# Projection fill written ahead of the rows in the differential-attention units of a Trainium2 block kernel

## The chip, the cores and the metric

The kernel is one program on one core of a Trainium2 chip. A core has engines with instruction streams of their own: TensorE (PE, with its weight loads shown as PEld), VectorE (DVE), ScalarE (ACT), GpSimd (POOL) and SyncE (SP), which here issues nearly all DMAs. The metric is the device time of one execution in microseconds (us), as the median of several runs.

## The reference

One decoder block with S = 1024 tokens and width 1024. A normalised input is projected; 8 forgetting-attention (FoX) heads and 4 differential-attention heads run over the projections; their outputs are gated, projected, merged by sigmoid gates, projected again and added to the input. The part in which the change lies is the differential attention:

```python
qd = apply_rope(qb.reshape(b, s, DIFF_HEADS, 2, DIFF_QK_DIM).transpose(0, 2, 3, 1, 4), cos, sin)
kd = apply_rope(kb.reshape(b, s, DIFF_HEADS, 2, DIFF_QK_DIM).transpose(0, 2, 3, 1, 4), cos, sin)
# diff_attention, for a block i of 128 query rows:
logits = jnp.einsum('bhmqd,bhmkd->bhmqk', qi, k).astype(jnp.float32) * scale
logits = jnp.where(kpos[None, :] <= qpos[:, None], logits, -jnp.inf)
p = jax.nn.softmax(logits, axis=-1)
pd = p[:, :, 0] - lam * p[:, :, 1]
return jnp.einsum('bhqk,bhkd->bhqd', pd.astype(v.dtype), v)
```

FoX attention is alike, with one softmax per head and a cumulated forget term added to the logits.

## The kernel before

All values are fp32. For TensorE each is split into a high and a low part in fp32r, and each matrix product is done as three products (high by high, high by low, low by high); a projection chunk of 512 columns is 24 matmuls. The phases follow one another on the clock: the normalised input and the value projections up to about 107 us, the projections of the first unit up to 131 us, then eight attention units, then gates, branch products and output products to the end.

A unit is a differential head (units 0 to 3) or a pair of FoX heads (units 4 to 7). A unit has groups of two rows, a row being 128 queries. For a differential row the function `row` asks for the swapped copies X of the query operand (L473, DMAs from SP), calls `s_row` for each of the two softmaxes (score matmuls L492 and L493 into a PSUM tile `Sd`; a DVE read of that tile with mask and running extreme into `Pd` and `mxd`, L495; an exponential on ACT, L501), takes the reciprocals `l` (DVE, L591), scales the second softmax on POOL (L592) and the first on ACT (L594), and adds them on POOL (L595). A group's `products` are built by `av`: transposes of `Pd` on PE into `ptd` (L522), a cast on ACT into `phd` (L525), the low part on DVE into `pld` (L526), the products with V on PE into `ypd` (L546), and an evacuation. Row i of a unit has (i+1) x 128 columns, and a score tile at most 512, so late rows cost more; the four groups g = 0 to 3 carry the weights 3, 7, 11 and 15, of 36.

Beside its rows and products each unit has a `fill`: the projections of the next unit, cut into chunks (k and q, two each), a z chunk (`pz`), and from unit 3 on sums of squares (`ssq`). A projection loads its weights by a DMA (L314, `raw_k` and the like), splits them on POOL (`hi_k`, L321) and DVE (`lo_k`, L324), runs 24 matmuls (L334) into one of two PSUM tiles `pk`, `pq` or `pz`, and for a differential unit goes through a rotation (`rope`): a copy on ACT (L362), four DMAs for the swapped halves (L366), a product on DVE (L368) and one on POOL (`swk`, `swq`, L369), their sum on DVE (L370), and the stacking into TA, TB, KA, KB (L378 to L382 with DMAs; L384 to L387 in unit 0). How much of the fill is taken behind a group goes by the weights done so far: units 0 and 1 have 6 tasks and take 1, 1, 2, 2; unit 2 has 4 and takes 1 each; unit 3 has 9 and takes 1, 2, 3, 3.

The pools that bear on the order: three PSUM tiles for scores, two for projections, two for transposes and one for `ypd`; two buffers each for the raw, high and low weights; a pool of three large buffers that holds the rotation tables and the mask and later the forget rows `cb` of FoX units (`cb` is loaded at L578 and trimmed on POOL at L618).

The written order of a unit's group n is: rows of n, products of group n-1, share n of the fill. This is not the order of execution. The code is recorded and a list scheduler in the tool chain then sets each engine's instruction order by a simulated timeline, with the written order as priority. Two things written the other way round can therefore come out interleaved in many ways, and a change at one place moves instructions on every engine behind it.

Of the kernel before, what the change touches and what calls it, by code (L numbers as in the profile page):

```python
# [50 lines left out]
def tile_hybrid_block(  # L51
# [288 lines left out]
    with ExitStack() as st:  # L340
# [75 lines left out]
        def z_tasks(t):  # L416
            return spill_tasks(f"z{t}", (ZA + t * P) if t < 4 else (ZB + (t - 4) * P), z_d[t])
# [20 lines left out]
        def sum_squares(t, c):  # L438

            sl = slice(c * CH, (c + 1) * CH)  # L440
            sq = stg.tile([P, CH], F32, tag="raw", name=f"sq{t}_{c}", bufs=4)
            nc.sync.dma_start(sq, y_d[t][:, sl])
            nc.scalar.activation(sq, sq, AF.Square)
            hi, lo = (stg.tile([P, CH], F32R, tag="sw", name=f"sq{part}{t}_{c}") for part in range(2))
            nc.scalar.copy(hi, sq)
            nc.gpsimd.tensor_tensor(lo, sq, hi, op=ALU.subtract)
            ps = pj.tile([P, CH], F32, tag="pj", name=f"ssq{t}_{c}")[0:32]
            nc.tensor.matmul(ps, lhsT=onesr, rhs=hi, start=True, stop=False)
            nc.tensor.matmul(ps, lhsT=onesr, rhs=lo, start=False, stop=True)
            nc.scalar.copy(sq[0:1], ps[0:1])  # L450
            nc.sync.dma_start(ss_d[t:t + 1, sl], sq[0:1])

        def subln_scales(t):
            rs = sub_rs[:, t]
            nc.sync.dma_start(rs, ss_d[t].rearrange("(p j) -> p j", j=8))
            rstd_of(rs, rs, P, SUB_EPS)
            nc.sync.dma_start(rs_d[t].rearrange("(p j) -> p j", j=8), rs)
# [96 lines left out]
        def products(trans, prod, g):  # L554
            for jj in range(g + 1 + SKEW):
                if jj <= g:
                    trans(jj)
                if jj >= SKEW:
                    prod(jj - SKEW)
# [91 lines left out]
        def forget_sums():  # L651

            fgf = fg.rearrange("p a b -> p (a b)")
            fs = pp.tile([P, 4, 64], F32, tag="P", name="fs")
            fn, fe, fu, fc = (fs[:, n, :] for n in range(4))
            nc.vector.tensor_scalar(fn, fgf, -1.0, None, op0=ALU.mult)
            nc.vector.tensor_tensor(fn, fn, fgf, op=ALU.min)
            nc.scalar.activation(fe, fn, AF.Exp)
            nc.vector.tensor_scalar(fu, fe, 1.0, None, op0=ALU.add)
            nc.vector.tensor_scalar(fc, fu, -1.0, None, op0=ALU.add)  # L660
            nc.vector.tensor_tensor(fc, fe, fc, op=ALU.subtract)
            nc.scalar.activation(fn, fu, AF.Ln)
            nc.vector.reciprocal(fu, fu)
            nc.vector.tensor_tensor(fc, fc, fu, op=ALU.mult)
            nc.vector.tensor_tensor(fn, fn, fc, op=ALU.add)
            nc.vector.tensor_scalar(fe, fgf, 0.0, None, op0=ALU.min)
            nc.vector.tensor_tensor(fe, fe, fn, op=ALU.subtract)
            lf = pp.tile([8, S], F32, tag="P", name="lf")
            cum = pp.tile([8, S], F32, tag="P", name="cum")
            ones8 = pp.tile([8, S], F32, tag="P", name="ones8")  # L670
            nc.gpsimd.memset(ones8, 1.0)
            for half in range(2):
                tp = tps.tile([P, CH], F32, tag="tp", name=f"ft{half}")
                for q in range(4):
                        b = half * 4 + q
                        nc.tensor.transpose(tp[0:8, q * P:(q + 1) * P], fe[:, b * 8:(b + 1) * 8], ident)
                nc.scalar.copy(lf[:, half * CH:(half + 1) * CH], tp[0:8, :])
            nc.vector.tensor_tensor_scan(cum, ones8, lf, initial=0.0, op0=ALU.mult, op1=ALU.add)
            nc.vector.tensor_scalar(cum, cum, -8.0, None, op0=ALU.mult)
            nc.sync.dma_start(cum_d, cum)  # L680
# [7 lines left out]
        for u in range(8):  # L688
            load, load_v, groups = nxt or unit_attn(u, T)
            nxt = None  # L690
            if u == 0:
                vload.append(load_v)
            if u == 1:
                forget_sums()
            load()
            fill = []
            if u + 1 < 8:
                T, tasks = unit_proj(u + 1)
                fill += tasks
            for t in ZFILL[u]:  # L700
                fill += z_tasks(t)
            for t in SFILL[u]:
                fill += [lambda t=t, c=c: sum_squares(t, c) for c in range(2)]
                fill.append(lambda t=t: subln_scales(t))
            late = [fill.pop(), gate[0]] if u == 7 else []
            total = sum(s[0] for s in groups)
            done, nf = 0, 0
            for n, (wgt, rws, prd) in enumerate(groups):
                if n == len(groups) // 2 and u < 7:
                    nxt = unit_attn(u + 1, T)  # L710
                    vload.append(nxt[1])
                for r in rws:
                    r()
                mark = lasts[0]
                if pend and (u < 7 or n <= TAIL):
                    products(*pend())
                if u == 7 and n >= TAIL:
                    tail.append(prd)
                pend = prd
                done += wgt  # L720
                while nf < len(fill) and nf < len(fill) * done * (3 if u == 7 else 1) / total:
                    fill[nf]()
                    nf += 1
                if u == 7:
                    for f, a, b in LATE[n]:
                        with tc.issue_after(mark):
                            late[f](range(a, b))
                    if n == GFILL:
                        break
# [503 lines left out]
```

## Time and profile before

| what | value |
|---|---|
| runs | 900.85, 901.63, 899.52 us; median 900.85 |
| profiled execution | 899.54 us, of which the span of the trace is 897.8 |
| granted TensorE clock, mean | 0.998 |
| first differential unit (0) | about 131 to 181 us of the span |
| units 1 and 2, and the start of 3 | 181 to 297 us |
| rest of unit 3 | 297 to 333 us |
| FoX units 4 to 7 | 333 to 582 us and a little beyond |
| gates, branch and output products | 582 us to the end |

The profiled execution is 1.74 us longer than its span and 1.31 us below the median of the three runs. Where the profile gives a row `[x <-engine ...]`, x is the idle time in front of that instruction and what follows the arrow is what ended it. PEld is the part of TensorE that loads weights ahead of the matmuls: it can wait while earlier matmuls still run, so a wait shown on PEld is more than what the matmuls lose by it.

### The profile page before, as it was taken

How to read it: one execution, taken by the hardware profiler on the slowest of the kernel's cores; microseconds unless marked ns; L12 is line 12 of the kernel's file. 1: busy time of each engine (PE TensorE's matmuls, PEld its weight loads, DVE VectorE, ACT ScalarE, POOL GpSimd, SP SyncE). 2: the span in 40 equal slices, each digit the busy share in tenths (PEclk: the TensorE clock that was granted, in tenths of full speed). 3: DMA queues.
4: the chain of work that ended last, by engine and by line, in shares of the span. 5: the costliest groups of instructions: out<-in, count | busy, mean ns of one | idle time of the engine just before them, and what ended most of it. 6: DMA issues, size and time to landing. Idle time of an engine off the chain costs nothing.

```text
span 897.8 us, 13825 instructions
## 1 busy us (share of the span) xinstructions
PE 881.9 (98%) x4612; PEld 746.7 (83%) x4612; DVE 580.4 (65%) x1124; ACT 429.0 (48%) x864; POOL 408.9 (46%) x401
## 2 busy tenths in 40 slices
PE   8999999999999999999999999999999999999997
PEld 6999987788888888888888888888888888888885
DVE  6666555767666744456647556626776897648896
ACT  7423224665756654365545646624453362314352
POOL 2234224645646535254344435426534323483963
PEclk9999999999999999999999999999999999999999
DMA  8576656756657763635636430297766599210495
GB/s 306 188 254 245 215 164 158 179 137 170 155 137 184 183 177 77 187 94 133 188 94 155 141 106 30 88 411 240 235 202 213 168 359 312 78 41 1 123 197 172
DMA packets 138186, 154.81 MB, mean 172 GB/s; under 512 B 12145, under 2 KB 98161, under 8 KB 137090
## 3 DMA queue, kind: packets, MB, share of 16 engines
q1 hardware_dynamic: 133744, 151.55, 56.1%
q0 software_dynamic: 4224, 2.10, 2.1%
q8 instruction: 37, 0.61, 0.3%
q14 instruction: 35, 0.29, 0.1%
q10 hardware_dynamic: 146, 0.27, 0.1%
HBM read 86.17 MB, written 38.34 MB: 139 GB/s over the span
## 4 chain that ended last, share of the span: by engine, by line
PE 87%; DMA 3%; DVE 3%; SPq 2%; ACT 2%; POOL 2%; issue 1%; POOLq 0%; DVEq 0%; ACTq 0%
PE x_g L830 15%; PE pv L214 10%; PE pb L990 10%; PE pz L334 9%; PE x_o L830 8%; PE pk L334 7%; PE pq L334 7%; PE ypf L546 3%; PE ptf L522 3%; PE ypd L546 2%; PE Sf L492 2%; PE Sf L493 2%; PE ptd L522 1%; PE Sd L492 1%; PE Sd L493 1%
## 5 line engine op out<-in xcount | busy, mean ns | idle before, releaser
L214 PE MATMUL pv<-wvhi,hT 128*128 128x264 f32 (+2 forms) x384 | 88.6, 325 | 0.0
L334 PE MATMUL pq<-hT,hi_q 128*128 128x512 f32 x256 | 82.1, 395 | 0.0
L334 PE MATMUL pz<-hT,hi_z 128*128 128x512 f32 x256 | 81.6, 394 | 0.4 <-DVE rotq L368 0.3
L334 PE MATMUL pk<-hT,hi_k 128*128 128x512 f32 x256 | 81.7, 393 | 0.0
L990 PE MATMUL pb<-yT,hi_br 128*128 128x512 f32 x256 | 79.0, 389 | 0.0
L830 PE MATMUL x_g<-T,a_g 128*128 128x512 f32 x336 | 78.0, 391 | 0.0
L830 PE MATMUL x_o<-wo_op,a_o 128*128 128x512 f32 x324 | 74.8, 392 | 0.0
L830 PEld LDWEIGHTS x_g<-T,a_g 128*128 128x128 f32 x336 | 63.1, 188 | 13.8
L830 PEld LDWEIGHTS x_o<-wo_op,a_o 128*128 128x128 f32 x324 | 60.7, 188 | 13.9 <-DVE a_o L767 0.5
L214 PEld LDWEIGHTS pv<-wvhi,hT 128*128 128x128 f32 x384 | 64.8, 192 | 5.7
L526 DVE TENSOR_TENSOR plf<-ptf,phf 128x512 fp32r<-128x512 f32 (+1 forms) x80 | 50.1, 635 | 25.1 <-ACT phf L525 24.4
L501 ACT ACTIVATE Pd<-Pd,mxd 128x128 f32<-128x128 f32 (+7 forms) x64 | 49.8, 779 | 33.4 <-DVE mxd L495 33.3
L618 POOL TENSOR_TENSOR cb<-cb,trim 128x128 f32<-128x128 f32 x64 | 29.3, 462 | 74.6 <-DVE mxf L495 51.6
L214 PE MATMUL pv<-wvlo,hT 128*128 128x256 f32 (+2 forms) x192 | 61.7, 326 | 0.0
L501 ACT ACTIVATE Pf<-Pf,mxf 128x1024 f32<-128x1024 f32 (+3 forms) x64 | 49.8, 779 | 24.5 <-DVE mxf L495 22.4
L830 PE MATMUL x_g<-hT,a_g 128*128 128x512 f32 x252 | 59.1, 392 | 0.0
L623 POOL TENSOR_SCALAR Pf<-Pf,lf 128x1024 f32<-128x1024 f32 (+3 forms) x64 | 47.9, 753 | 20.9 <-DVE lf L622 17.6
L525 ACT CAST phf<-ptf 128x512 fp32r<-128x512 f32 (+1 forms) x80 | 42.6, 543 | 30.7 <-PE ptf L522 26.4
L990 PEld LDWEIGHTS pb<-yT,hi_br 128*128 128x128 f32 x256 | 48.0, 188 | 10.4 <-issue 0.4
L830 PEld LDWEIGHTS x_g<-hT,a_g 128*128 128x128 f32 x252 | 47.3, 188 | 10.4
L334 PEld LDWEIGHTS pz<-hT,hi_z 128*128 128x128 f32 x256 | 47.3, 188 | 9.5 <-DVE rotq L368 0.6
L334 PEld LDWEIGHTS pq<-hT,hi_q 128*128 128x128 f32 x256 | 47.2, 188 | 8.9
(277 smaller groups left out, 2289.2 us busy)
## 6 DMA issues: line engine op xcount, KB each, us to landing
t_d<-t SPq DMA_DIRECT2D x16, 512.0 KB, 4.0
T<-t_d SPq DMA_DIRECT2D x8, 1024.0 KB, 11.0
raw<-in_w_in_dram SPq DMA_DIRECT2D x14, 512.0 KB, 5.5
vb_d<-vbs SPq DMA_DIRECT2D x8, 512.0 KB
va_d<-vas SPq DMA_DIRECT2D x8, 512.0 KB, 3.8
raw_k<-in_w_in_dram SPq DMA_DIRECT2D x8, 512.0 KB, 4.4
raw_q<-in_w_in_dram SPq DMA_DIRECT2D x8, 512.0 KB, 4.7
V<-vb_d SPq DMA_DIRECT2D x4, 1024.0 KB, 6.2
```

The lines of the kernel that those rows point to most:

```text
L214: nc.tensor.matmul(ps[n], lhsT=hT[hp][k // 4][i // 4][:, k % 4, hs], rhs=wt[k][:, a:b], start=first, stop=(k == KT - 1 and hp == 1))
L334: mm = nc.tensor.matmul(ps, lhsT=a[:, k, :], rhs=hT[h][k // 4][c][:, k % 4, :], start=(k == 0 and a is hi and h == 0), stop=(k == KT - 1 a ...
L492: nc.tensor.matmul(ps, lhsT=A[:, qs], rhs=B[:, a:b], start=True, stop=False)
L501: nc.scalar.activation(pr[:, 0:n], pr[:, 0:n], AF.Exp, bias=mx[:, len(pcs) - 1:len(pcs)], scale=-1.0, accum_out=le)
L522: lasts[0] = nc.tensor.transpose(pt[:, o * P:(o + 1) * P], rows[2 * g + r][:, j * P:(j + 1) * P], ident).ins
L525: nc.scalar.copy(ph[:, 0:n], pt[:, 0:n])
L526: nc.vector.tensor_tensor(pl[:, 0:n], pt[:, 0:n], ph[:, 0:n], op=ALU.subtract)
L546: lasts[0] = nc.tensor.matmul(o, lhsT=a, rhs=b[:, src], start=(j == 0 and n == 0), stop=(odd == 1 and jj == g and n == len(prods) - 1)).ins
L618: nc.gpsimd.tensor_tensor(diag, diag, trim, op=ALU.add)
L623: held[0] = nc.gpsimd.tensor_scalar(p1[:, 0:n], p1[:, 0:n], l1, 1.0, op0=ALU.mult, op1=ALU.mult).ins
L830: nc.tensor.matmul(x[m], lhsT=a[:, ai, k, :], rhs=right[m][bi][k], start=(k == 0 and n == 0), stop=(k == 3 and n == 2))
L990: nc.tensor.matmul(ps, lhsT=a[:, kk, :], rhs=yT[g][h][:, k % 2, sl], start=(k == 0 and a is hi and h == 0), stop=(k == 3 and a is lo))
```

## The change

For units 0 to 3 the share of the fill that belongs to a group is written in front of the group's rows. The sum of the weights done is raised earlier, so the share itself is the same, and the second call behind the products then finds nothing left. For units 4 to 7 the written order is the one of before. A unit's written order becomes: fill 0, rows 0, products of the unit before; fill 1, rows 1, products 0; and so on. Between units 3 and 4 the fill of unit 3 now stands before its last rows, and the fill of unit 4 still behind its first.

```diff
--- before.py
+++ after.py
@@ -709,6 +709,16 @@
                 if n == len(groups) // 2 and u < 7:
                     nxt = unit_attn(u + 1, T)
                     vload.append(nxt[1])
+                done += wgt
+
+                def more(nf):
+                    while nf < len(fill) and nf < len(fill) * done * (3 if u == 7 else 1) / total:
+                        fill[nf]()
+                        nf += 1
+                    return nf
+
+                if u < 4:
+                    nf = more(nf)
                 for r in rws:
                     r()
                 mark = lasts[0]
@@ -717,10 +727,7 @@
                 if u == 7 and n >= TAIL:
                     tail.append(prd)
                 pend = prd
-                done += wgt
-                while nf < len(fill) and nf < len(fill) * done * (3 if u == 7 else 1) / total:
-                    fill[nf]()
-                    nf += 1
+                nf = more(nf)
                 if u == 7:
                     for f, a, b in LATE[n]:
                         with tc.issue_after(mark):
```

Nothing is added or removed on any engine: the number of PE, DVE, ACT, POOL and SP instructions and their shapes are the same. The order of all engines is the same up to about 131 us and from about 629 us of the time before, and differs between.

The first place is VectorE in unit 0, around rows 4 and 5 (`loq1_0` and `rotk1_1` belong to the projection of unit 1). `Pd0_1_4<-Sd0_1_4_0` is the read of the first score tile of row 4, second softmax, of unit 0; `lo_k2` is the low part of the key weights of unit 2. Before:

```order
L379 TENSOR_TENSOR loq1_0_1657<-rotq1_0_1652,hiq1_0_1656 128x512
L495 ISA Pd0_1_4_1684,mxd0_1_4_1685<-Sd0_1_4_0_1686,dmask_168 128x384
L495 ISA mxd0_1_4_1685 128x1
L368 TENSOR_TENSOR rotk1_1_1791<-pk1_1_1759,cosT_166 128x512
L495 ISA Pd0_1_4_1684,mxd0_1_4_1685<-Sd0_1_4_1_1690,dmask_168,mxd0_1_4_1685 128x256
L495 ISA mxd0_1_4_1685 128x1
L495 ISA Pd0_0_5_1700,mxd0_0_5_1701<-Sd0_0_5_0_1702,dmask_168 128x512
L495 ISA mxd0_0_5_1701 128x1
L591 RECIPROCAL l0_4_1672<-l0_4_1672 128x2
L495 ISA Pd0_0_5_1700,mxd0_0_5_1701<-Sd0_0_5_1_1706,dmask_168,mxd0_0_5_1701 128x256
L495 ISA mxd0_0_5_1701 128x1
L324 TENSOR_TENSOR lo_k2_2163<-raw_k2_2160,hi_k2_2162 128x1024
```

and after:

```order
L495 ISA Pd0_0_4_1761,mxd0_0_4_1762<-Sd0_0_4_0_1763,dmask_168 128x384
L495 ISA mxd0_0_4_1762 128x1
L495 ISA Pd0_1_4_1772,mxd0_1_4_1773<-Sd0_1_4_0_1774,dmask_168 128x384
L495 ISA mxd0_1_4_1773 128x1
L324 TENSOR_TENSOR lo_k2_2056<-raw_k2_2053,hi_k2_2055 128x1024
L495 ISA Pd0_0_4_1761,mxd0_0_4_1762<-Sd0_0_4_1_1767,dmask_168,mxd0_0_4_1762 128x256
L495 ISA mxd0_0_4_1762 128x1
L526 TENSOR_TENSOR pld0_1_0_1817<-ptd0_1_0_1815,phd0_1_0_1816 128x512
L526 TENSOR_TENSOR pld0_1_1_1826<-ptd0_1_1_1824,phd0_1_1_1825 128x384
L495 ISA Pd0_1_4_1772,mxd0_1_4_1773<-Sd0_1_4_1_1778,dmask_168,mxd0_1_4_1773 128x256
L495 ISA mxd0_1_4_1773 128x1
L495 ISA Pd0_0_5_1788,mxd0_0_5_1789<-Sd0_0_5_0_1790,dmask_168 128x512
```

`lo_k2`, which needs `raw_k2` from a DMA and `hi_k2` from POOL, stood behind all reads of row 4 and the first softmax of row 5, and now stands ahead of two of row 4's four reads.

The second place is GpSimd at the end of unit 2, rows 6 and 7 and the trims of the forget rows. Before:

```order
L321 TENSOR_SCALAR hi_q4_3453<-raw_q4_3451 128x1024
L592 TENSOR_SCALAR Pd2_1_6_3105<-Pd2_1_6_3105,l2_6_3093,nlam_85 128x896
L595 TENSOR_TENSOR Pd2_0_6_3094<-Pd2_0_6_3094,Pd2_1_6_3105 128x896
L369 TENSOR_TENSOR swq3_1_3222<-swq3_1_3222,sinT_167 128x512
L592 TENSOR_SCALAR Pd2_1_7_3132<-Pd2_1_7_3132,l2_7_3120,nlam_85 128x1024
L618 TENSOR_TENSOR cb4_0_3849<-cb4_0_3849,trim_74 128x128
L595 TENSOR_TENSOR Pd2_0_7_3121<-Pd2_0_7_3121,Pd2_1_7_3132 128x1024
L592 TENSOR_SCALAR Pd3_1_0_3257<-Pd3_1_0_3257,l3_0_3249,nlam_85 128x128
L618 TENSOR_TENSOR cb4_1_3851<-cb4_1_3851,trim_74 128x128
```

and after:

```order
L369 TENSOR_TENSOR swq3_1_3114<-swq3_1_3114,sinT_167 128x512
L592 TENSOR_SCALAR Pd2_1_5_3039<-Pd2_1_5_3039,l2_5_3027,nlam_85 128x768
L595 TENSOR_TENSOR Pd2_0_5_3028<-Pd2_0_5_3028,Pd2_1_5_3039 128x768
L618 TENSOR_TENSOR cb4_0_3849<-cb4_0_3849,trim_74 128x128
L618 TENSOR_TENSOR cb4_1_3851<-cb4_1_3851,trim_74 128x128
L592 TENSOR_SCALAR Pd2_1_6_3149<-Pd2_1_6_3149,l2_6_3137,nlam_85 128x896
L595 TENSOR_TENSOR Pd2_0_6_3138<-Pd2_0_6_3138,Pd2_1_6_3149 128x896
L592 TENSOR_SCALAR Pd2_1_7_3176<-Pd2_1_7_3176,l2_7_3164,nlam_85 128x1024
L595 TENSOR_TENSOR Pd2_0_7_3165<-Pd2_0_7_3165,Pd2_1_7_3176 128x1024
```

The two trims, each of which needs a DMA (`cb`), stood between the scaling and the sum of row 7 and behind row 0 of the next unit; they now stand together ahead of row 6.

The third place is TensorE in unit 3, where `pq4_1` is a projection of unit 4 and `Sd3_0_5_0` a score tile of row 5. Before:

```order
L492 MATMUL Sd3_1_4_1_3549<-KB3_2678,TB3_2676 128x256
L493 MATMUL Sd3_1_4_1_3549<-KB3_2678,X1d3_2_3528 128x256
L522 MATMUL ptd3_1_0_3586<-ident_69,Pd3_0_2_3396 128x128
L492 MATMUL Sd3_0_5_0_3561<-KA3_2677,TA3_2675 128x512
L493 MATMUL Sd3_0_5_0_3561<-KA3_2677,X0d3_2_3524 128x512
L334 MATMUL pq4_1_3618<-hT101_95,hi_q4_3453 128x512
L334 MATMUL pq4_1_3618<-hT001_91,lo_q4_3454 128x512
L522 MATMUL ptd3_1_0_3586<-ident_69,Pd3_0_3_3415 128x128
```

and after:

```order
L522 MATMUL ptd3_1_1_3690<-ident_69,Pd3_0_3_3487 128x128 x2
L492 MATMUL Sd3_1_4_1_3644<-KB3_2678,TB3_2676 128x256
L493 MATMUL Sd3_1_4_1_3644<-KB3_2678,X1d3_2_3623 128x256
L492 MATMUL Sd3_0_5_0_3656<-KA3_2677,TA3_2675 128x512
L493 MATMUL Sd3_0_5_0_3656<-KA3_2677,X0d3_2_3619 128x512
L492 MATMUL Sd3_0_5_1_3660<-KA3_2677,TA3_2675 128x256
L493 MATMUL Sd3_0_5_1_3660<-KA3_2677,X0d3_2_3619 128x256
L546 MATMUL ypd3_1_3680<-phd3_1_0_3682,V3_2948 128x256 x2
L492 MATMUL Sd3_1_5_0_3667<-KB3_2678,TB3_2676 128x512
L493 MATMUL Sd3_1_5_0_3667<-KB3_2678,X1d3_2_3623 128x512
L492 MATMUL Sd3_1_5_1_3671<-KB3_2678,TB3_2676 128x256
L493 MATMUL Sd3_1_5_1_3671<-KB3_2678,X1d3_2_3623 128x256
```

Rows 4 and 5 were interleaved with the 24 matmuls of `pq4_1`; now that fill (and `pz2_0`, `pz2_1`) stands ahead, and the rows 4 to 7 follow each other, with only transposes, products and four `ssq` matmuls between, until `pk5_0` begins.

## Prediction

> **What bounds the kernel now.** The head of the page came first, then the chain that ended last.
>
> ```profile
> span 897.8 us, 13825 instructions
> PE 881.9 (98%) x4612; PEld 746.7 (83%) x4612; DVE 580.4 (65%) x1124; ACT 429.0 (48%) x864; POOL 408.9 (46%) x401
> PE 87%; DMA 3%; DVE 3%; SPq 2%; ACT 2%; POOL 2%; issue 1%; POOLq 0%; DVEq 0%; ACTq 0%
> ```
>
> TensorE is busy for 98% of the span. The change removes no matmul, so it can win only idle time of TensorE and lose only by making more. The next view is the windows by stage: start and end, length, then busy time of PE, PEld, DVE, ACT and POOL, the granted clock, the DMA share and GB/s.
>
> ```profile
> 131.00:181.00 50.00, 47.21 (x237) 38.37 (x236) 34.98 (x82) 26.22 (x56) 27.02 (x24) 1.00 0.69 174
> 181.00:259.00 78.00, 78.00 (x437) 67.43 (x437) 52.42 (x133) 50.56 (x110) 40.75 (x36) 1.00 0.58 145
> 259.00:297.00 38.00, 37.54 (x206) 31.86 (x206) 25.78 (x63) 23.53 (x50) 23.52 (x21) 1.00 0.72 184
> 297.00:333.00 36.00, 35.84 (x196) 29.87 (x195) 21.37 (x54) 19.58 (x40) 13.72 (x12) 1.00 0.71 187
> 333.00:582.00 249.00, 246.36 (x1436) 213.44 (x1435) 143.33 (x395) 135.80 (x296) 111.24 (x157) 1.00 0.44 116
> ```
>
> In the differential units TensorE idles 50 - 47.21 = 2.79 us in unit 0, nothing in unit 1 and the first half of 2, 0.46 around the end of unit 2 and 0.16 at the end of unit 3: 3.41 in all. The FoX units idle 2.64. The waits of the weight loads say what the idle of unit 0 is (us in total, times, longest), and the timeline of PEld gives single ones there and at the end of unit 2:
>
> ```profile
> PEld ptd L522 <- POOL Pd L595: 2.5, 3, 1.3
> PEld Sd L493 <- DMA X1d<-TB: 1.3, 1, 1.3
> PEld pz L334 <- DVE rotq L368: 0.6, 1, 0.6
> PEld Sd L492 <- DVE mxd L495: 0.5, 1, 0.5
> PEld pz L334 <- DVE rotk L368: 0.3, 1, 0.3
> ```
>
> ```profile
> 138.28 0.19 PEld L493 LDWEIGHTS Sd<-KB,X1d 128*128 128x128 f32 x1 [1.26 <-DMA X1d<-TB]
> 148.43 0.14 PEld L522 LDWEIGHTS ptd<-ident,Pd 128*128 128x128 f32 x1 [0.81 <-POOL Pd L595]
> 159.49 0.53 PEld L522 LDWEIGHTS ptd<-ident,Pd 128*128 128x128 f32 x5 [1.34 <-POOL Pd L595]
> 285.72 0.19 PEld L492 LDWEIGHTS Sd<-KB,TB 128*128 128x128 f32 x1 [0.79 <-DVE mxd L495]
> 289.72 0.42 PEld L522 LDWEIGHTS ptd<-ident,Pd 128*128 128x128 f32 x4 [0.35 <-POOL Pd L595]
> ```
>
> A weight load runs ahead of its matmul, so a wait on PEld costs less than it shows. The price of that lead is one matmul: the chain has 24 of 512 columns in 5.49 us, 0.23 each.
>
> ```profile
> 107.55 5.49 PE pk L334 x24
> ```
>
> Taking 0.23 off each of the seven waits of unit 0 leaves 5.2 - 1.6 = 3.6 us lost; the two at the end of unit 2 leave 0.56 + 0.12 = 0.7. The windows, in which a stretched matmul counts as busy, say 2.79 and 0.46. I sum by waits less 0.23.
>
> **The change, part by part.** Work is only moved: each matmul, read and DMA is issued as often as before, so each moved step costs its wait and what it blocks.
>
> *A, unit 0.* These rows, from the page's groups, the chain, the timelines of SP, POOL and DVE and the groups of line 324, carry the terms.
>
> ```profile
> L526 DVE TENSOR_TENSOR plf<-ptf,phf 128x512 fp32r<-128x512 f32 (+1 forms) x80 | 50.1, 635 | 25.1 <-ACT phf L525 24.4
> ...
> 129.01 8.77 DMA V<-vb_d
> 156.41 0.59 SPq L314 DMA_DIRECT2D raw_k<-in_w_in_dram  x1
> 154.88 1.91 POOL L369 TENSOR_TENSOR swq<-swq,sinT 128x512 f32<-128x512 f32 x1 [0.49 <-DMA swq<-rawq]
> 156.78 1.31 POOL L592 TENSOR_SCALAR Pd<-Pd,l,nlam 128x512 f32<-128x512 f32 x1
> 158.17 1.27 POOL L595 TENSOR_TENSOR Pd<-Pd,Pd 128x512 f32<-128x512 f32 x1
> 160.89 1.06 POOL L321 TENSOR_SCALAR hi_k<-raw_k 128x1024 fp32r<-128x1024 f32 x1 [1.45 <-DMA raw_k<-in_w_in_dram]
> 163.69 2.42 POOL L595 TENSOR_TENSOR Pd<-Pd,Pd 128x640 f32<-128x640 f32 x1
> 160.99 0.47 DVE L495 CUSTOM_DVE_ANT_0 Pd<-Sd,dmask,mxd 128x256 f32<-128x256 f32 x1
> L324 DVE TENSOR_TENSOR lo_k<-raw_k,hi_k x8: 1210/1224/1686, 98.4 to 427.0; 128x1024 fp32r<-128x1024 f32 x8
> ```
>
> The X1d wait (1.03 after the deduction) ends with a small DMA that stands in SP's queue behind the load of V, 8.77 us in the chain. The change leaves that pair in place, and TensorE reaches the tile one matmul earlier: 1.26. The row-0 wait (0.81, and the 0.3 that is left of the 2.5 behind it) ends with GpSimd's sum; a whole projection chunk now stands ahead of the transposes, so about 0. Row 3's wait of 1.34 is GpSimd's order: the rotation product `swq` (1.91) ran just before row 3's scaling and sum. The new order takes the scaling first, so I take 0.5 of the 1.1. The load of the z weights moves behind the next V in SP's queue; its matmuls are still more than a chunk of 5.49 us away, which hides it. The two z waits on rotations (0.45) go too, since the rotation now has longer.
>
> Against that, `lo_k2` now blocks VectorE with two score tiles of row 4 unread. It needs the load (issued 156.41, landed by 160.89), the split on GpSimd (1.06) and itself (1.22), so it ends at about 163.2 where the reads behind it could start at about 160.8: 2.4 us. TensorE meanwhile has the two freed tiles to fill and transposes, about 1.3 us, so 1.1 is lost on score tiles; that includes the 0.27 of before. Queued behind `lo_k2` are also the low parts `pld` of the first products, which have chunks ahead of them. And row 4's own transposes come 5.3 us of matmuls (counted at 0.23 per 512 columns) after its last score matmul instead of 12.1. From the last read to the finished sum took 160.99 to 166.11, 5.1 us; two `pld` now stand between row 4's reads, at 0.635 by the group above: 6.4, with hand-overs 6.5, so 1.2 lost. Sum after: 1.26 + 0.5 + 1.1 + 1.2 = 4.06 against 3.6, so +0.4. If none of the three new waits comes it is 1.26 - 3.6 = -2.3. If the load keeps GpSimd for 1 us more (it kept it for 1.45) and a sum takes 2.42 instead of 1.27, it is 0.4 + 0.95 + 1.15 = +2.5. I take the worked value, since its rows are the same instructions.
>
> *B, the end of unit 2.*
>
> ```profile
> 281.33 0.55 SPq L578 DMA_DIRECT2D cb<-cum_d  x1
> 282.84 0.61 SPq L578 DMA_DIRECT2D cb<-cum_d  x1
> 276.49 1.09 POOL L592 TENSOR_SCALAR Pd<-Pd,l,nlam 128x896 f32<-128x896 f32 x1 [1.94 <-DVE l L591]
> 283.71 1.21 POOL L592 TENSOR_SCALAR Pd<-Pd,l,nlam 128x1024 f32<-128x1024 f32 x1 [0.91 <-DVE l L591]
> 286.85 0.46 POOL L618 TENSOR_TENSOR cb<-cb,trim 128x128 f32<-128x128 f32 x1 [1.93 <-DMA cb<-cum_d]
> ```
>
> GpSimd held row 7's sum behind a trim that waited 1.93 us for its DMA; that gave both waits at 285.72 and 289.72. The trims now stand between rows 5 and 6. Rows are scaled 7.2 us apart there, the loads follow the last use of the rotation table, which has moved forward as well, and they need about 5.5 from 281.33 to 286.85. Then two trims of 0.46 fit into GpSimd's own wait for `l`. Behind the trims only row 6's scaling and sum are queued. So -0.7, with bounds -0.7 and +1.0 (a trim that keeps row 6 waiting for half of the 1.93).
>
> Unit 1 and the first half of unit 2 I cost at nothing: 78.00 of 78.00 us are busy, and a group still has at least a chunk of 5.49 us between its rows and its transposes; without it row 4's 1.2 us of unit 0 is the nearest price.
>
> *C, unit 3.* Rows 4 to 7 now come in one burst of 15 score tiles before `pk5_0`. Reads of tiles, by shape (minimum, median, maximum ns, in the last 35 us of the unit):
>
> ```profile
> L495 DVE CUSTOM_DVE_ANT_0 Pd<-Sd,dmask x8: 544/684/692, 300.6 to 330.5; 128x512 f32<-128x512 f32 x6, 128x384 f32<-128x384 f32 x2
> L495 DVE CUSTOM_DVE_ANT_0 Pd<-Sd,dmask,mxd x8: 475/548/751, 302.5 to 332.2; 128x256 f32<-128x256 f32 x4, 128x384 f32<-128x384 f32 x2, 128x512 f32<-128x512 f32 x2
> ```
>
> VectorE: seven tiles of 512 columns at 0.68, four of 384 at 0.54, four of 256 at 0.48 make 8.8 us, 10.1 with two `pld`. TensorE: 24 matmul equivalents (5.5), and transposes, products and `ssq` at the same price per column, about 8.5. Three tiles of lead are worth 2.0, so the reads keep up (10.1 - 2.0 - 8.5 = -0.4) while the lead is full; it isn't where a row begins behind a product, and I take +0.2. Bounds: -0.2, and +1.4 if a weight split of 1.22 falls in between.
>
> *D, FoX units.* Nothing is written differently, yet the scheduler's order is new there. The one place where I see a price is the start of unit 7:
>
> ```profile
> 537.52 0.19 PEld L492 LDWEIGHTS Sf<-KB,TB 128*128 128x128 f32 x1 [0.78 <-DVE mxf L495]
> ```
>
> There a score tile is now wanted after four matmuls of 512 columns instead of eight, 0.92 less cover. Half of it is +0.4. The rest of the new order may save half of the 2.64 idle, or double it: -1.3 to +2.6.
>
> Sum: +0.4 - 0.7 + 0.2 + 0.4 = +0.3. The profiled execution (899.54, of which 897.8 span and 1.74 around it) would become 899.8. It stands 1.31 below the median of 900.85; the median should be about **901.2**.
>
> *A rule against the change.* VectorE operations with two SBUF inputs lengthen here beside GpSimd: two rotation sums of one shape took 0.69 and, while a GpSimd sum ran, 2.32.
>
> ```profile
> 156.82 0.69 DVE L370 TENSOR_TENSOR rotq<-rotq,swq 128x512 f32<-128x512 f32 x1 [1.18 <-POOL swq L369]
> ...
> 271.32 2.32 DVE L370 TENSOR_TENSOR rotk<-rotk,swk 128x512 f32<-128x512 f32 x1 [1.81 <-POOL swk L369]
> 271.26 1.83 POOL L595 TENSOR_TENSOR Pd<-Pd,Pd 128x768 f32<-128x768 f32 x1
> ```
>
> [...]
>
> **The rivals.** *Faster: the fill covers the waits.* With a chunk of 5.49 us ahead of each group, everything that TensorE waits for in units 0 to 3 could be hidden. For it speaks that two of the largest waits, rows 0 and 3, end on GpSimd sums. Against it: X1d is a DMA behind V, and fill taken before row 4 is no longer there after it. It wins at most the 3.41 us of idle: 900.85 - 3.4 = 897.4.
>
> *Slower: the score tiles become the bound.* The fill no longer separates rows, VectorE needs 0.68 per tile where TensorE needs 0.46, and three tiles are the lead. It decides once VectorE has more than 2.0 us of other work among the reads of a burst. Price: the upper ends in unit 0 (+2.5) and unit 3 (+1.4), less 0.7 in unit 2 and with +0.4 in unit 7: +3.6, 904.5.
>
> [...] If `lo_k2` and the `lo` sums behind it meet the sums of rows 3 and 4, each is longer by those 2.32 - 0.69 = 1.6 us. Two of them in unit 0 with the tiles waiting are +3.2 on the forecast's +0.3 less the 1.1 already counted: +2.4, 903.2.
>
> That nothing moves is excluded: the orders differ over 450 us.
>
> **How the numbers follow.** Within 0.2% is 1.8 us, about what a measurement of this kernel can tell from no change: 899.05 to 902.65. The forecast, gains and losses in balance, holds 46% (40 within, 4 faster, 2 slower, from the bounds of A and D); the cover 28% (24 faster, 4 within, where only a part is hidden); the tiles 17%, all slower; the port 9% (5 slower, 4 within). That gives 28% faster, 48% within, 24% slower. The range goes down to the cover's 897.4 and up to the tiles' 904.5, which leaves out the tails of each; the forecast's own is 899.0 to 903.0.
>
> **What would show it.** Right: in unit 0 an X1d wait of about 1.3, no wait of row 0, new waits of `ptd` on row 4 and of `Sd` on `mxd` behind `lo_k2`; no waits at the end of unit 2 and trims that wait while GpSimd has nothing else; FoX idle between 2 and 4. Wrong: a unit 0 whose idle falls under 1.5 (cover), score waits over 2 us in unit 3 (tiles), or FoX idle moved by more than everything in the differential units.

## The result: 1.1% slower, and the profile after

The median of six runs is 910.08 us against 900.50 us before; the ratio is 1.011, with a 95% interval of 1.0083 to 1.0137. The runs spread more than those of before: 907.33 to 913.32, against 899.03 to 901.63. The profiled execution took 911.23 us with a span of 909.5, so 11.7 us more span than before. All rows down to the experiments are of this execution, except where they are said to be of before. The head of the page and the chain that ended last:

```profile
span 909.5 us, 13817 instructions
PE 886.7 (97%) x4612; PEld 750.6 (83%) x4612; DVE 584.4 (64%) x1124; ACT 429.7 (47%) x864; POOL 413.0 (45%) x401
PE 85%; DMA 6%; ACT 2%; DVE 2%; issue 2%; POOL 1%; SPq 1%; POOLq 0%; DVEq 0%; ACTq 0%
```

DMA has gone from 3 to 6% of the chain. The windows by stage, in the same columns as before (the granted clock is the third number from the end):

```profile
131.00:181.00 50.00, 45.75 (x218) 37.54 (x217) 30.39 (x71) 22.57 (x50) 24.42 (x22) 0.97 0.70 176
181.00:259.00 78.00, 75.57 (x401) 63.89 (x400) 54.48 (x122) 46.31 (x96) 39.41 (x31) 0.98 0.54 134
259.00:297.00 38.00, 35.69 (x192) 30.68 (x191) 23.98 (x58) 19.57 (x41) 18.92 (x16) 0.96 0.69 177
...
333.00:345.00 12.00, 10.53 (x52) 7.81 (x51) 7.51 (x25) 11.74 (x24) 6.61 (x6) 1.00 0.37 94
345.00:593.00 248.00, 246.17 (x1447) 213.82 (x1446) 146.84 (x403) 137.12 (x297) 114.49 (x157) 1.00 0.43 116
```

Between 131 and 297 us TensorE now idles 4.25 + 2.43 + 2.31 = 8.99 us, where it idled 2.79 + 0 + 0.46 = 3.25. And the granted clock is no longer 1.00. The waits of the weight loads from 131 to 333 us and the stops of PE in its timeline:

```profile
PEld Sd L492 <- DVE mxd L495: 4.2, 4, 2.5
PEld pk L334 <- ACT sz L433: 2.5, 2, 2.2
PEld ptd L522 <- POOL Pd L595: 2.5, 2, 2.0
PEld pz L334 <- DVE rotk L368: 2.0, 1, 2.0
PEld Sd L493 <- DMA X1d<-TB: 1.1, 1, 1.1
```

```profile
159.56 0.77 PE L522 MATMUL ptd<-ident,Pd 128*128 128x128 f32 x5 [1.78 <-POOL Pd L595]
162.09 0.73 PE L334 MATMUL pz<-hT,hi_z 128*128 128x512 f32 x2 [1.76 <-DVE rotk L368]
236.34 0.72 PE L334 MATMUL pk<-hT,hi_k 128*128 128x512 f32 x2 [1.95 <-ACT sz L433]
291.40 0.45 PE L492 MATMUL Sd<-KB,TB 128*128 128x384 f32 x1 [2.31 <-DVE mxd L495]
334.42 0.51 PE L546 MATMUL ypd<-phd,V 128*128 128x256 f32 x2 [1.25 <-ACT phd L525]
```

Five stops, each ended by a different line, in all four units (the wait on `X1d` was there before, 1.26 us against 1.10 now). Windows of 1 us just behind the second, third and fourth:

```profile
163.00:164.00 1.00, 1.00 (x4) 0.79 (x3) 1.00 (x1) 0.00 (x0) 0.00 (x0) 0.50 1.04 230
239.00:240.00 1.00, 1.00 (x4) 0.71 (x4) 1.00 (x1) 0.00 (x0) 0.00 (x0) 0.50 0.95 353
293.00:294.00 1.00, 1.00 (x4) 0.72 (x3) 0.86 (x3) 1.00 (x3) 0.83 (x1) 0.50 0.79 139
```

The clock is 0.50 there. The trace's clock records give three stretches, from 162.7, 237.8 and 292.4 us, each 3.41 us long; before has none until the kernel's last few microseconds (0.50 from 894 to 897 us). Matmuls of 512 columns began 0.43 us apart in the first (three in the 1.28 us from 163.01), against the 0.23 of the chain of before. Half of three times 3.41 is 5.1 us of lost work, an estimate by the clock; by the 0.43 it is 4.8. With the 5.7 us of added idle that is 10.8 of the 11.7 us. The end of unit 3 adds 1.5 us of idle (the stop at 334 us above all), and the FoX units idle 1.83 us of 248, against 2.64 of 249.

**One cause behind the different names.** What stands in front of the releasers, engine by engine (timelines of SP, POOL, DVE and ACT; unit 0, then 1, then 2). "issue" means that the profile shows nothing that the engine waited for; the cast at 234.37 starts as the rotation sum that it reads ends:

```profile
153.64 1.04 POOL L321 TENSOR_SCALAR hi_z<-raw_z 128x1024 fp32r<-128x1024 f32 x1 [2.58 <-DMA raw_z<-in_w_in_dram]
157.01 1.28 POOL L369 TENSOR_TENSOR swq<-swq,sinT 128x512 f32<-128x512 f32 x1 [0.50 <-DMA swq<-rawq]
158.25 1.26 POOL L595 TENSOR_TENSOR Pd<-Pd,Pd 128x512 f32<-128x512 f32 x1
158.32 1.73 DVE L370 TENSOR_TENSOR rotq<-rotq,swq 128x512 f32<-128x512 f32 x1 [2.38 <-POOL swq L369]
161.35 0.68 DVE L368 TENSOR_TENSOR rotk<-pk,cosT 128x512 f32<-128x512 f32 x1
```

```profile
232.28 1.29 POOL L369 TENSOR_TENSOR swq<-swq,sinT 128x512 f32<-128x512 f32 x1 [4.44 <-DMA swq<-rawq]
233.59 0.69 DVE L370 TENSOR_TENSOR rotq<-rotq,swq 128x512 f32<-128x512 f32 x1 [4.59 <-POOL swq L369]
234.37 0.62 ACT L378 CAST hiq<-rotq 128x512 fp32r<-128x512 f32 x1 [4.23 <-issue]
235.73 0.56 ACT L433 COPY sz<-pz 128x512 f32<-128x512 f32 x1
```

```profile
283.19 4.07 SPq L366 DMA_DIRECT2D swq<-rawq  x3
288.75 1.26 POOL L369 TENSOR_TENSOR swq<-swq,sinT 128x512 f32<-128x512 f32 x1 [5.30 <-DMA swq<-rawq]
290.04 0.69 DVE L370 TENSOR_TENSOR rotq<-rotq,swq 128x512 f32<-128x512 f32 x1 [5.28 <-POOL swq L369]
290.65 0.68 DVE L495 CUSTOM_DVE_ANT_0 Pd<-Sd,dmask 128x512 f32<-128x512 f32 x1
```

Each time the rotation of the next unit's queries waits for its swap DMAs, and the waiting instruction stands in an engine's order ahead of what TensorE needs. In unit 0 GpSimd's row-3 sum stands behind `swq`, and `rotk`, which gives the projection tile back to `pz`, behind the rotation sum. The z load held GpSimd before that (2.58 us), but the swap, for which it then waited 0.50 us more, landed only at 157.01. In unit 1 ScalarE's copy `sz`, which gives a tile back to `pk`, stands behind the cast of the rotated queries. In unit 2 a score read stands behind the sum while VectorE idles for 5.28 us. The waits of VectorE for the rotations of queries and keys from 131 to 333 us, before and then after:

```profile
DVE rotq L370 <- POOL swq L369: 13.2, 6, 5.2
DVE rotk L370 <- POOL swk L369: 9.0, 7, 3.0
```

```profile
DVE rotq L370 <- POOL swq L369: 21.9, 7, 5.3
DVE rotk L370 <- POOL swk L369: 5.2, 5, 1.8
```

Together they go from 22.2 to 27.1 us. Such waits were there before, and as long; but what TensorE lost behind one of them then was at most 0.90 us, at 159.50 in unit 0, and nothing in unit 1. The stop at 334 us has the same form on ScalarE, where the cast `phd` stands behind the squares of the first unit's output, which wait for a load:

```profile
333.26 0.63 ACT L443 ACTIVATE sq<-sq 128x512 f32<-128x512 f32 x1 [1.55 <-DMA sq<-y_d]
```

### The profile page after: what moved, and what is told of

Read it like the earlier page. It is cut to its first block, busy times and chain, and to the rows that moved or that the text cites. A ratio compares the mean times of both kernels' runs of the same rounds, so it can differ in the third digit from the quotient of the medians.

```text
span 909.5 us, 13817 instructions
## 1 busy us (share of the span) xinstructions
PE 886.7 (97%) x4612; PEld 750.6 (83%) x4612; DVE 584.4 (64%) x1124; ACT 429.7 (47%) x864; POOL 413.0 (45%) x401
## 4 chain that ended last, share of the span: by engine, by line
PE 85%; DMA 6%; ACT 2%; DVE 2%; issue 2%; POOL 1%; SPq 1%; POOLq 0%; DVEq 0%; ACTq 0%
PE x_g L837 15%; PE pb L997 10%; PE pv L214 9%; PE pz L334 8%; PE x_o L837 8%; PE pk L334 8%; PE pq L334 7%; PE ypf L546 4%; PE ptf L522 3%; PE ypd L546 2%; PE Sf L492 2%; PE Sf L493 2%; DMA swq<-rawq 1%; PE pg L334 1%; PE ptd L522 1%
## 5 line engine op out<-in xcount | busy, mean ns | idle before, releaser
L334 PE MATMUL pz<-hT,hi_z 128*128 128x512 f32 x256 | 84.2, 401 | 1.8 <-DVE rotk L368 1.8
L592 POOL TENSOR_SCALAR Pd<-Pd,l,nlam 128x128 f32<-128x128 f32 (+7 forms) x32 | 33.3, 1041 | 53.9 <-DVE l L591 35.2
L334 PEld LDWEIGHTS pk<-hT,hi_k 128*128 128x128 f32 x256 | 47.6, 190 | 12.0 <-ACT sz L433 2.5
```

Source lines behind the costliest of these rows:

```text
L334: mm = nc.tensor.matmul(ps, lhsT=a[:, k, :], rhs=hT[h][k // 4][c][:, k % 4, :], start=(k == 0 and a is hi and h == 0), stop=(k == KT - 1 a ...
L592: nc.gpsimd.tensor_scalar(p2[:, 0:n], p2[:, 0:n], l2, nlam, op0=ALU.mult, op1=ALU.mult)
```

## The experiments

Theory A: TensorE stops behind instructions that wait for a DMA, above all the rotation, and a stop of about 2 us is followed by half clock, as those of 1.95 and 2.31 us in units 1 and 2 were. Its rivals are named in the expectations, each written ahead of its run. Lines left out of a diff are marked by dots.

### One unit at a time

```diff
-                if u < 4:
+                if u == 0:
```

The other three kernels have 1, 2 and 3 in place of the 0.

> The fill is written ahead in unit 0 alone. Theory A (TensorE stops because VectorE and ScalarE stand in order behind a rotation sum, L370, that waits for its swap DMAs, and a stop of about 2 us is followed by 3.4 us at a granted clock of 0.5): in the changed kernel unit 0 has two stops of 1.78 us and one stretch of half clock, and lost about 1.5 us more than before between 130 and 190 us; so about +1.5 us, 902. Theory B (score tiles are the bound where rows follow each other without fill): unit 0 has only row 4 in a row, so within 1 us of before. Theory C (the loss arises only where the new order of one unit meets that of the next): nearly nothing alone.

> The fill is written ahead in unit 1 alone. Theory A: in the changed kernel the stop of 1.95 us in front of pk at 236 us, with VectorE idle for 4.59 us before a rotation sum and a stretch of half clock behind it, makes unit 1 the dearest, about 4.7 us of excess between 190 and 250 us; so about +4.5 us, 905, if the stop is found again. Theory B: about +1.5, since its rows 4 to 7 still have fill of z between them. Theory C: under 1 us.

> The fill is written ahead in unit 2 alone. Theory A: the stop of 2.31 us in front of the score matmuls at 291 us, with VectorE idle for 5.28 us before a rotation sum and half clock behind it, cost 2.7 us more than before between 250 and 300 us; so about +2.7 us, 903. Theory B: about +1. Theory C: under 1 us.

> The fill is written ahead in unit 3 alone, whose fill are FoX projections, which have no rotation. Theory A: no long stop behind a rotation can come, no stretch of half clock; +1 to +2 us from the 1.25 us stop in front of the products at 334 us, 902. Theory B: this is the unit with the longest burst of score tiles, so the largest share of the 9.6 us, +3 or more, 904. Theory C: under 1 us.

Measured beside 899.49 us for before: unit 0 alone 909.75 (ratio 1.0112, 1.0093 to 1.0131), unit 1 alone 905.81 (1.0064, 1.0044 to 1.0083), unit 2 alone 897.78 (0.9981, 0.9970 to 0.9992), unit 3 alone 901.74 (1.0022, 1.0008 to 1.0035). The sum would be 17 us, not 9.6: no theory had that, and A's times for units 0 and 2 (902 and 903) were wrong as well. The order is drawn anew for everything behind the first difference, so a unit's change is paid in other units too. Unit 0 alone has a stop and half clock at 161.6 us, and again at 294.7 us, around the end of unit 2, which is written as before; there GpSimd's sum of row 6 stands behind a trim that waits 1.94 us for its DMA. Unit 1 alone came out at A's 905 by luck: the stop that A put at 236 us is 1.03 us at 231 us, without half clock, and the loss lies in unit 2, behind a rotation sum for which VectorE waited 4.81 us (the stop below, one of 1.56 us at 288.41, and half clock from 289.0 us):

```profile
285.90 0.49 PE L492 MATMUL Sd<-KA,TA 128*128 128x512 f32 x1 [1.79 <-DVE mxd L495]
```

Unit 3 alone, which I expected to be free of half clock, has a stretch at 325.1 us, behind a wait on the squares:

```profile
324.41 0.42 PE L448 MATMUL ssq<-sq,onesr 128*32 128x512 f32 x1 [1.77 <-ACT sq L445]
```

There ScalarE waited 1.49 us for the DMA of the squares' input: A's form with another DMA, though A as put had no half clock in this kernel. Theory B (score tiles) falls: the unit with the longest burst of score tiles is the cheapest but one. Unit 2 alone is faster; its idle between 131 and 297 us is 2.42 where before has 3.25:

```profile
131.00:297.00 166.00, 163.58 (x874) 138.05 (x873) 112.75 (x272) 97.45 (x207) 89.52 (x77) 1.00 0.66 166
```

### The swap off the DMA queues

The four swap DMAs and the copy ahead of them become four copies of 32 partitions on ScalarE, from PSUM:

```diff
...
-                nc.scalar.copy(raw, ps)
...
                 for b in range(4):
                     o = b ^ 1
-                    nc.sync.dma_start(sw[b * 32:(b + 1) * 32, :], raw[o * 32:(o + 1) * 32, :])
+                    nc.scalar.copy(sw[b * 32:(b + 1) * 32, :], ps[o * 32:(o + 1) * 32, :])
```

> The changed kernel, with the swapped halves of the rotation written by four copies of 32 partitions on ScalarE straight from the PSUM tile, in place of one copy to SBUF and four DMAs on SP; the rest is computed as before. Theory A (TensorE stops behind a rotation sum that waits for its swap DMAs): the waits of VectorE on the rotation sum fall from 21.9 us to under 8, no stretch of half clock is left in the units, and the time falls to 898 to 902. Theory B (score tiles bound where rows follow each other): ScalarE gets about 16 x 1.6 us more work and the stops stay, 908 to 912.

> The kernel before, with the same four copies on ScalarE in place of the copy and the swap DMAs. Theory A: its rotation waits (13.2 us on VectorE) were nearly all covered, so only the waits of unit 0 shrink: 897 to 900, and within 3 us of the changed kernel with the same copies. Theory B: no faster than before, 900 or more, and 8 to 10 us ahead of the changed kernel with the same copies.

The changed kernel with these copies takes 898.95 us (0.9987 of before, 0.9978 to 0.9997), the kernel before with them 893.71 (0.9925, 0.9912 to 0.9938). This is the fastest version that was run, 0.75% under before. No stretch of half clock is left in the units of either, and VectorE waits 2.8 us (the changed kernel) and 3.1 us for rotations. Their windows from 131 to 297 us, the changed kernel second:

```profile
131.00:297.00 166.00, 166.00 (x905) 143.11 (x904) 117.58 (x285) 126.29 (x258) 93.16 (x79) 1.00 0.57 144
```

```profile
131.00:297.00 166.00, 166.00 (x891) 142.44 (x890) 111.06 (x273) 123.07 (x250) 91.87 (x78) 1.00 0.58 144
```

TensorE has no idle left in units 0 to 2, with the fill ahead or behind. So the whole loss of this stretch, 5.7 us of idle and 5.1 us of half clock, went with the swap's DMAs; the order is drawn anew by this edit too, but the four kernels of the next section, with four more orders, show the same 166.00. But A promised the two kernels within 3 us and they are 5.2 apart. The windows from 297 to 345 us show where a part of it is, 2.89 us of idle against 0.22 (before with the copies, then the change with them, and its waits there; the lines are two lower in these kernels):

```profile
297.00:345.00 48.00, 47.78 (x252) 40.02 (x251) 24.38 (x68) 27.94 (x53) 26.61 (x24) 1.00 0.55 147
```

```profile
297.00:345.00 48.00, 45.11 (x242) 36.93 (x241) 24.74 (x69) 29.71 (x57) 26.80 (x24) 1.00 0.51 138
```

```profile
PEld ssq L446 <- ACT sq L443: 2.5, 2, 1.3
PEld pk L334 <- ACT sq L448: 1.2, 1, 1.2
```

Not all of this is a wait for a DMA: at 326.72 us the cast that TensorE waits for stands behind four exponentials on ScalarE, which is busy from 322.82 us on.

### What remains with the copies

The same copies, with the fill ahead in units 0 to 2, in unit 2, in unit 0 and in unit 1 alone.

> The swap copies on ScalarE, and the fill ahead in units 0, 1 and 2 but not 3. With these copies the fill ahead in all four units gave 898.95 and none 893.71. Theory D (what is left of the cost sits at the end of unit 3, where the sums of squares now stand ahead of the last rows and TensorE waits for their squares: 2.9 us for ssq and 1.4 us for pk behind it in that trace): 893 to 895.5. Rival E (the rest comes from all units, a little each, as score tiles follow each other): 897 to 898.

> The swap copies on ScalarE, and the fill ahead in unit 2 alone, which without these copies was 1.7 us faster than before. If that gain was the trims of the forget rows moved off the sum of row 7, which has nothing to do with the swap: 892 (1.7 under 893.7). If it was fewer waits on rotations: no gain, 893.7.

> Fill ahead in unit 0 alone, with the swap copies on ScalarE. Theory A (the cost is the rotation's wait for its swap): the 10.1 us fall to under 3 against the kernel before with the same copies (893.7), so 893 to 897, no stretch of half clock in the units. Rival E (the order of rows and fill costs by itself): 900 or more.

> Fill ahead in unit 1 alone, with the swap copies on ScalarE. Theory A: the 6.3 us fall to under 3, so 893 to 897. Rival E: 898 or more.

Measured: 898.53 (0.9980, 0.9968 to 0.9992), 895.55 (0.9947, 0.9926 to 0.9968), 897.91 (0.9985, 0.9976 to 0.9994), 897.30 (0.9979, 0.9970 to 0.9987). Theory D falls: without unit 3's change the remainder stays. The gain of unit 2 alone is gone too, but that says nothing on the trims: in the kernel before with the copies they already stand ahead of row 6's sum, at 273.58 and 275.43 us. Beyond the 0.8 us of idle, that gain stays open. For units 0 and 1 the truth lies between the theories: against before with the copies (0.9925) they cost 0.6 and 0.5%, where without the copies they cost 1.1 and 0.6%; for unit 1 hardly anything is recovered. Rival E as I put it, rows that follow each other in these units, isn't it either, since all four have 166.00 busy of 166.00 between 131 and 297 us. The remainder lies behind 297 us, where the new order falls differently. Counted by the columns of the matmuls begun, the trace of the kernel with all four units is 0.5 us behind that of before with the copies at 297 us, 5.1 us at 345 and 6.2 at 600. So most of it arises at the end of unit 3, also without unit 3's change: unit 0 alone and unit 1 alone lose 3.3 and 4.1 us there. Idle is 2.7 of the 4.6 us in the kernel with all four; what the rest is stays open.

### The rotation's end written behind the rows

```diff
-                nc.gpsimd.tensor_tensor(sw, sw, sinT[:, sl], op=ALU.mult)
-                nc.vector.tensor_tensor(rot, rot, sw, op=ALU.add)
-                return rot
+                def finish():
+                    nc.gpsimd.tensor_tensor(sw, sw, sinT[:, sl], op=ALU.mult)
+                    nc.vector.tensor_tensor(rot, rot, sw, op=ALU.add)
+                    return rot
+                return finish
...
```

`finish` and the stacking are called behind the rows that are written next.

> The changed kernel, with the second half of each rotation (the product with the sine on GpSimd, the sum, the split and the stacking) written behind the rows of its group; the matmuls, the copy, the swap DMAs and the product with the cosine stay ahead. Theory A: the score reads now come before the waiting sum in VectorE's order, so the waits on the rotation that stop TensorE go: 899 to 903. Theory B: the rows still follow each other without fill, 907 or more.

> The kernel before, with the second half of each rotation written behind the rows of the next group. Theory A: a small gain where a rotation sum held VectorE in unit 0, 896 to 901. Theory B: the same time as before, 900.

The changed kernel so takes 903.50 us (1.0043, 1.0027 to 1.0059), a little above the range; the kernel before takes 905.36 (1.0058, 1.0042 to 1.0075), a miss for every theory. Written later is not executed later: the first still has the two stops of unit 0 (1.54 and 1.76 us) and a stretch of half clock behind them. In the second VectorE's longest wait for a rotation is now the one below, and two stretches of half clock follow stops in units 1 and 2 (lines here are two higher).

```profile
276.60 0.69 DVE L372 TENSOR_TENSOR rotk<-rotk,swk 128x512 f32<-128x512 f32 x1 [6.44 <-POOL swk L371]
```

### Other queues

```diff
-                    nc.sync.dma_start(sw[b * 32:(b + 1) * 32, :], raw[o * 32:(o + 1) * 32, :])
+                    nc.scalar.dma_start(sw[b * 32:(b + 1) * 32, :], raw[o * 32:(o + 1) * 32, :])
```

```diff
-                nc.sync.dma_start(f32(vt), src)
+                nc.scalar.dma_start(f32(vt), src)
```

> The changed kernel, with the four swap DMAs of each rotation issued from ScalarE's queue behind the copy that they read, instead of from SP's. Theory G (the swaps wait in SP's queue): the rotation waits of VectorE fall from 21.9 to under 12 us, no or one stretch of half clock, 899 to 903. Rival H (the DMA round trip itself is too long for the place that the order gives the sum): 906 or more, two or more stretches of half clock over the runs.

> The kernel before, with the swap DMAs issued from ScalarE's queue. Theory G: 896 to 899, most of the 6.3 us that the copies on ScalarE gained. Rival H: 899 to 902.

> The changed kernel, with the loads of V issued from ScalarE's queue, the swaps on SP as before. If it is V's completion that holds the swaps in SP's queue (in the changed kernel a swap stood 2.3 us at about 284 us and 1.3 us at 152 us): 901 to 905, and each group of four swaps is issued in under 3 us. If V is not the cause: 908 or more.

> The kernel before, with the loads of V issued from ScalarE's queue. The wait on X1d at 138 us, behind V's load, should shrink: 898 to 900.5. If V's issue holds ScalarE instead: over 901.

With the swaps on ScalarE's queue: 909.94 (1.0124, 1.0104 to 1.0145) and 906.13 (1.0078, 1.0058 to 1.0097). The two theories share the first: VectorE's waits for rotations fall from 27.1 to 8.7 us, as G said, but the time and the two stretches of half clock are H's. The wait has moved to ScalarE, where the issue of four swaps now takes 6.11 us and holds what stands behind it:

```profile
227.31 6.11 ACTq L366 DMA_DIRECT2D swq<-rawq  x4
233.46 0.83 ACT L594 ACTIVATE Pd<-Pd,l 128x640 f32<-128x640 f32 x1 [6.78 <-DMA swq<-rawq]
```

So the slow swaps are not a matter of SP's queue alone. The kernel before so changed lies above both forecasts; VectorE stood still for 6.83 us there, as the landing was no nearer:

```profile
276.41 1.26 POOL L369 TENSOR_TENSOR swk<-swk,sinT 128x512 f32<-128x512 f32 x1 [5.96 <-DMA swk<-rawk]
277.70 2.00 DVE L370 TENSOR_TENSOR rotk<-rotk,swk 128x512 f32<-128x512 f32 x1 [6.83 <-POOL swk L369]
```

With V on ScalarE's queue: 918.85 (1.0218, 1.0202 to 1.0235) and 913.05 (1.0162, 1.0145 to 1.0179). V's issue now stands ahead of ScalarE's copy of the first unit's projection, which comes 3.8 us later than in the kernel before; VectorE's product that gives a tile back stands behind the rotation sum, and TensorE waits 4.52 us for that tile at 128.45 us (rows of the kernel before so changed):

```profile
115.76 1.03 ACTq L571 DMA_DIRECT2D V<-vb_d  x2
116.83 0.59 ACT L362 COPY rawk<-pk 128x512 f32<-128x512 f32 x1 [9.09 <-issue]
```

So these two say nothing on whether V delays the swaps on SP; why three of them took 4.07 us to issue at 283 us in the changed kernel, and landed late, stays open.

### A stop made on purpose

Between two projections at 113 us, where TensorE is busy throughout, stands a transpose that waits for a chain of copies on ScalarE, of one (a range of 0) or of five (a range of 4, shown):

```diff
...
+                    nc.scalar.copy(gt, kps[0])
+                    for _ in range(4):
+                        nc.scalar.copy(gt, gt)
...
+                    tr = nc.tensor.transpose(tp[:, 0:P], gt[:, 0:P], ident).ins
...
```

The rows are of the short stop, then of the long one, then a window of the long one.

> The kernel before, with TensorE held once on purpose at about 113 us, where it is busy throughout: between the first key and query projections of unit 0 stands a transpose that waits for a copy on ScalarE (its output is used by nothing). Theory A: a stop of about 1.4 us costs itself and is followed by a granted clock of 1.0: 901.5. Rival F (any stop over a microsecond is followed by half clock): 1.4 + 1.7, 903.2.

> As the short stop, with four more copies in the chain, a stop of about 3.6 us. Theory A: it is followed by a stretch of 3.4 us at a granted clock of 0.5, in which half of the work is lost, so 3.6 + 1.7 = 5.3 us more than before, 905.4. Rival F: the same. If the clock stayed at 1.0, 903.7.

```profile
115.17 0.33 PE L398 MATMUL gtp<-ident,gt 128*128 128x128 f32 x1 [2.02 <-ACT gt L394]
```

```profile
118.43 0.48 PE L398 MATMUL gtp<-ident,gt 128*128 128x128 f32 x1 [4.62 <-ACT gt L396]
```

```profile
120.00:121.00 1.00, 1.00 (x4) 0.81 (x3) 0.52 (x1) 0.00 (x0) 0.45 (x1) 0.50 0.00 0
```

The short stop came out at 2.02 us, and the clock stayed at 1.00; 904.32 us (1.0044, 1.0022 to 1.0066). The long one was 4.62 us and a stretch of 3.41 us at 0.50 began at 118.1 us; 907.64 (1.0080, 1.0058 to 1.0102). Both lie above every forecast. Against 900.33 us for before, the short one costs 2 us more than its stop, the long one 1 us more than its stop and its half clock; the order behind them is drawn anew as well, so these remainders say nothing on the stop. F falls: 2.02 us without half clock, where 1.95 us at 236 us had it. A's "about 2 us" is not what decides either: with unit 0 alone, one of 1.29 us at 294.27 us has the stretch from 294.7 us behind it. What decides is not shown.

## Why the prediction was wrong, point by point

The forecast was 901.2 us with a range to 904.5; it came out at 910.08. In the profiled execution, by stage, with 1.7 us for each stretch of half clock (the estimate by the clock):

| stage | forecast | added idle | half clock |
|---|---|---|---|
| A, unit 0 | +0.4 | 1.5 | 1.7 |
| unit 1 and the first half of unit 2 | 0 | 2.4 | 1.7 |
| B, end of unit 2 | -0.7 | 1.9 | 1.7 |
| C, unit 3 | +0.2 | 1.5 | 0 |
| D, FoX | +0.4 | -0.8 | 0 |

The step that failed is the price of each stage by the waits that TensorE shows in the old order: it put unit 1 at nothing and the end of unit 2 at a gain, where new stops behind the rotation's swap, and half clock behind them, cost 4.1 and 3.6 us.

- *A, unit 0: right that new waits take the place of the old, wrong in which.* The X1d wait and the vanished row-0 wait came as said. The wait behind `lo_k2` (1.1) did not: when VectorE reached it, at 162.90, TensorE had the 24 matmuls of `pz` to run. Row 4's transposes (1.2) show 0.44 on the weight loads at 172.94 and no idle of TensorE. What failed is row 3's 0.5, and that the two z waits would go "since the rotation now has longer". GpSimd's sum of row 3 still stands behind `swq`, 1.78 us; and the z wait became 1.76 us, behind a rotation sum that stood ahead of its releaser. (4.06 less 3.6 is +0.5, not +0.4; nothing hangs on it.)
- *Unit 1 "at nothing": the largest miss.* That 78.00 of 78.00 us were busy showed that the old order covered its waits, not that a new one would. VectorE waited 22.2 us for rotations in the trace of before, at most 5.2 at a time; I looked at TensorE's waits alone, and didn't price what stands behind these in the new order.
- *B, the trims: moved as said, but misread.* Of the two waits that I gave to the trim, only the one at 289.72 stands behind it, and TensorE lost under 0.1 us by it. The one at 285.72 ended with a score read that stood behind `loq`, which came late because the rotation sum had waited for its swap. So -0.7 had no ground, and the case that later cost so much was in view (rows of before):

```profile
284.26 1.19 DVE L379 TENSOR_TENSOR loq<-rotq,hiq 128x512 fp32r<-128x512 f32 x1 [0.66 <-ACT hiq L378]
285.38 0.28 DVE L495 CUSTOM_DVE_ANT_0 Pd<-Sd,dmask 128x128 f32<-128x128 f32 x1
```

- *C, unit 3: +0.2 forecast.* The 1.25 us at 334 us came from ScalarE's order; the score reads that I had counted, bounded at +1.4, gave TensorE no stop over 0.2 us there.
- *D, FoX: inside its bounds,* 0.8 us less idle instead of 0.4 more.
- *The clock was no term at all.* Profile and windows of before had 1.00 in all units, and the longest idle there was 0.90 us. Three stretches are 5.1 of the 11.7 us by that estimate. They go with a part of the spread: the runs of the changed kernel with a mean clock of 0.995 took 907.33 and 908.92 us, those with 0.991 and 0.992 took 912.82 and 913.32; by these clocks about 3 of the 5 us between them are lost clock (an estimate).
- *The rivals.* The cover did not come. The tiles fell with unit 3 alone. The port, with 9% in the forecast, is a term that no run shows. What the trace of before shows in its place is that rotation sums took 1.48 and 2.32 us beside GpSimd's row sums, and 0.69 or 0.70 beside its scalings, the one at 156.82 among them. A longer `lo_k` did not come where I put it: it took 1.22 us at 162.90 in the trace after, with GpSimd idle. The lengthening may have a part one step on: the rotation sum at 158.32, in front of the releaser of `pz`, took 1.73 us beside GpSimd's sum of row 3, where the one at 233.59 took 0.69 with GpSimd idle; no run separates that. The slower side was right, by a mechanism that was not among them.

## What to carry to other kernels

Where a scheduler sets the order, as here, moving one block draws the order of every engine anew: look in the new order, on each engine, for instructions that wait for a DMA, take the longest landing that the trace shows, and ask what that TensorE needs stands behind them, also in stages that show no wait today. A tuned order that covers such round trips is easily lost: of the eleven other versions tried here with the swap on DMAs, the change among them and the stops made on purpose aside, one gained 0.2% and ten lost 0.2 to 2.2%. Take the round trip out of the chain first: with the swap as engine copies every order tried was faster than the kernel before, by 0.1 to 0.75%.

## What was not expected of the hardware

A stop can cost more than its length: in the trace after, the stops of 1.78 and 1.76 us together, of 1.95 and of 2.31 us were each followed by 3.41 us at 0.50, with matmuls 0.43 us apart instead of 0.23, about 1.6 us of lost work each (an estimate from that spacing). Which stops have such a stretch behind them is not told by their length: 1.29 us at 294.27 us with unit 0 alone had one, 2.02 us in the short stop had none. Whether the stretches come and go between runs of one kernel, and so make the 6 us between the runs of the changed one, is not shown: their places are known for the profiled executions alone, and the kernel before scattered by 2.6 us in the runs beside the change and by 6.5 in 18 later ones, where its two slowest had the lowest mean clock, 0.996.
